# A chunked state-space scan: products of split operands for two plain ones, and 1/sqrt through Ln and Exp

## The chip, the cores and the metric

The kernel runs on one core of one Trainium2 chip. The metric is the device time of one execution in microseconds (us); lower is better. Five engines matter: TensorE (PE, with its weight loads listed as PEld), VectorE (DVE), ScalarE (ACT), GpSimd (POOL), and SyncE (SP), which issues the transfers.

## The reference

A decoder block on 512 positions of width 1024. The part that the change touches is the scan of a Mamba-2 mixer: 32 heads of 64 channels in 4 groups of 8 heads, state size 128, four chunks of 128 positions.

```python
scores = jnp.einsum('bclgn,bcsgn->bgcls', cc, bc)
mmat = scores[:, :, None] * segsum_decay(a_cs)
y_diag = jnp.einsum('bghcls,bcsghp->bclghp', mmat, x)
decay_states = jnp.exp(a_cs[..., -1:] - a_cs)
states = jnp.einsum('bcsgn,bghcs,bcsghp->bcghpn', bc, decay_states, x)
...
def step(h, inp):
    s_c, d_c = inp
    return h * d_c[..., None, None] + s_c, h
...
y_off = jnp.einsum('bclgn,bcghpn,bghcl->bclghp', cc, prev, jnp.exp(a_cs))
...
y = y.reshape(b, seq, D_INNER).astype(h.dtype) * jax.nn.silu(z)
y = rmsnorm(y.reshape(b, seq, SSD_GROUPS, D_INNER // SSD_GROUPS),
            ssd_norm_w.reshape(SSD_GROUPS, D_INNER // SSD_GROUPS))
```

`rmsnorm` multiplies by `rsqrt(mean(x * x) + 1e-5)`, here over the 512 channels of a group. All inputs and the output are float32.

## The kernel before

All activations are kept transposed: 128 channels on the partitions, 512 positions along the free dimension. A matrix is multiplied in units: `unit` loads one 128x1024 block of weights, splits it into a high and a low part (`load_unit`: a cast to float32r on ScalarE, line 141, and a subtraction on VectorE, line 142), and `mm3` adds three products for each of 8 blocks (high x high, high x low, low x high: lines 151, 152, 153), 24 products of 512 columns in all. `split` (lines 121 and 122) does the same for an activation tile.

The scan is `ssd_group(g)`, one generator per group; `run` draws the steps of a group and places units of other matrices between them as fillers (the projections of the next group, the branch product of the group before, the pooling branch). The order of a queue is then set by a scheduler over all instructions, which may move them on ScalarE, VectorE, GpSimd and SyncE; `urgent` gives weight loads a high priority. Buffers are drawn from lists in turn (`S`: 50 tiles of 128x512; `PU`: 3 and `PS`: 5 banks of the accumulator memory; `MT`: 3 decay tiles).

In a group: B is transposed (419) and copied (420) to `bk`; the four score blocks are computed (425). `prepare(c)`, called one chunk ahead, loads the decay rows (433), computes two small exponentials (435, 437), masks on GpSimd (438), does eight exponentials on ScalarE (442), multiplies by the scores (443), transposes x (446), and scales it to `xdt` (448) and, for the first three chunks, to `xd` (454). The chunk's own step multiplies the state (470), forms the chunk's state with one float32 product `st` (474, 128x128 by 128x512), updates it (478, 480, 482), does sixteen small products for the diagonal part (490), and adds, gates and squares on VectorE, ScalarE and GpSimd (497 to 514). `ssum` collects the sums of squares over the four tiles of a group. At the end of a group one float32 product with a matrix of ones (523) sums `ssum` over the partitions and spreads the result; Sqrt (525) and `reciprocal` (527) make `rg`, by which the gated tiles are scaled (532) and then split for the branch product.

ScalarE computes functions from a table; where the next function is in another table, a load (ACT_TABLE_LOAD) stands ahead of it. Silu, Exp, Sqrt and Sigmoid alternate in the scan.

Of the kernel before, what the change touches and what calls it, by code (L numbers as in the profile page):

```python
# [7 lines left out]
F32 = mybir.dt.float32  # L8
F32R = mybir.dt.float32r
AF = mybir.ActivationFunctionType  # L10
ALU = mybir.AluOpType

P = 128
T = 512
# [4 lines left out]
HG = 8  # L19
NC = 4  # L20
# [41 lines left out]
def block_kernel(tc, xT, crow, arow, par, adaT, wstart, wz, wx, wpool_in, wgate, wpw, wbs, wbp, wout, wup, wdn, out):  # L62
# [3 lines left out]
    with (  # L66
# [33 lines left out]
            return par_t[:rows, a:a + n]  # L100

        ident = sb.tile([P, P], F32, name="ident")
        ones = sb.tile([P, P], F32, name="ones")
        eps_t = sb.tile([P, 1], F32, name="eps_t")
        mod = sb.tile([P, 48], F32, name="mod")
        amod = sb.tile([P, 16], F32, name="amod")
# [11 lines left out]
        def split(src):  # L118

            hi, lo = S.get(F32R), S.get(F32R)  # L120
            act.copy(hi, src)
            dve.tensor_tensor(lo, src, hi.bitcast(F32), ALU.subtract)
            return hi, lo
# [25 lines left out]
        def mm3(ps, w, x, start, stop, t0=0, t1=T):  # L149
            (whi, wlo), (xhi, xlo) = w, x  # L150
            pe.matmul(ps, whi, xhi[:, t0:t1], start=start, stop=False)  # L151
            pe.matmul(ps, whi, xlo[:, t0:t1], start=False, stop=False)  # L152
            pe.matmul(ps, wlo, xhi[:, t0:t1], start=False, stop=stop)  # L153
# [256 lines left out]
        def ssd_group(g):  # L410
# [2 lines left out]
            v3 = lambda t: t.rearrange("p (a b) -> p a b", b=64)  # L413
            v4 = lambda t: t.rearrange("p (a b) -> p a b", b=P)
            cdg, decg = cd[g % 2], dec[g % 2]
            bk = S.get()
            ps = PS.get()
            for c in range(NC):
                pe.transpose(ps[:, c * P:(c + 1) * P], bT[:, c * P:(c + 1) * P], ident)
            act.copy(bk, ps)  # L420
            PS.put(ps)
            sc = PS.get()
            for c in range(NC):
# [5 lines left out]
            def prepare(c):  # L429

                cc = slice(c * P, (c + 1) * P)
                m = MT.get()
                sp.dma_start(m, cs_d[heads, cc].partition_broadcast(P))
                if c < 3:
                    act.activation(cdg[:, c, :], m[:, :, P - 1], AF.Exp)  # L435
                    dve.tensor_tensor(decg[:, c, :], m[:, :, P - 1], ncs[:, c, heads], ALU.add)
                    act.activation(decg[:, c, :], decg[:, c, :], AF.Exp)
                pool.affine_select(  # L438
                    m, m, pattern=[[0, HG], [1, P]], compare_op=ALU.is_ge, fill=-1e30, base=0,
                    channel_multiplier=-1)  # L440
                for i in range(HG):
                    act.activation(m[:, i, :], m[:, i, :], AF.Exp, bias=ncs[:, c, g * HG + i:g * HG + i + 1])  # L442
                dve.tensor_tensor(m, m, sc[:, cc].unsqueeze(1).broadcast_to([P, HG, P]), ALU.mult)
                ps = PS.get()
                for i in range(4):
                    pe.transpose(ps[:, i * P:(i + 1) * P], xs[:, i, cc], ident)
                xdt = S.get()
                dve.tensor_tensor(
                    v3(xdt), v3(ps), dtk[:, c, heads].unsqueeze(2).broadcast_to([P, HG, 64]), ALU.mult)
                PS.put(ps)  # L450
                xd = None
                if c < 3:
                    xd = S.get()
                    dve.tensor_tensor(
                        v3(xd), v3(xdt), decg[:, c, :].unsqueeze(2).broadcast_to([P, HG, 64]), ALU.mult)
                return m, xdt, xd

            ready = [prepare(0)]
# [1 line left out]
            for c in range(NC):  # L460
                cc = slice(c * P, (c + 1) * P)
                if c < NC - 1:
                    ready.append(prepare(c + 1))
                    yield
                m, xdt, xd = ready.pop(0)
                yo = None
                if c > 0:
                    yo = PS.get()
                    for i in range(4):
                        pe.matmul(yo[:, i * P:(i + 1) * P], prev[:, i * P:(i + 1) * P], cT[:, cc],  # L470
                                  start=True, stop=True)
                if c < 3:
                    st = PS.get()
                    pe.matmul(st, bk[:, cc], xd, start=True, stop=True)  # L474
                    S.put(xd)
                    nprev = S.get()
                    if c == 0:
                        act.copy(nprev, st)
                    else:
                        dve.tensor_tensor(  # L480
                            v3(nprev), v3(prev), cdg[:, c, :].unsqueeze(2).broadcast_to([P, HG, 64]), ALU.mult)
                        dve.tensor_tensor(nprev, nprev, st, ALU.add)
                        S.put(prev)
                    PS.put(st)
                    prev = nprev
                yd = PS.get()
                for i in range(4):
                    for hh in range(2):
                        o = 64 * hh
                        pe.matmul(  # L490
                            yd[o:o + 64, i * P:(i + 1) * P],
                            xdt[:, i * P + o:i * P + o + 64], m[:, 2 * i + hh, :], start=True, stop=True)
                MT.put(m)
                S.put(xdt)
                y = S.get()
                for i in range(4):
                    dve.scalar_tensor_tensor(
                        y[:, i * P:(i + 1) * P], xs[:, i, cc], col("dskip", 4 * g + i),
                        yd[:, i * P:(i + 1) * P], ALU.mult, ALU.add)
                PS.put(yd)  # L500
                if c > 0:
                    E = S.get()
                    for hh in range(2):
                        sp.dma_start(
                            v4(E)[64 * hh:64 * hh + 64],
                            ecs_d[heads, cc].rearrange("(i t) k -> t i k", t=2)[hh].partition_broadcast(64))
                    dve.tensor_tensor(E, yo, E, ALU.mult)
                    PS.put(yo)
                    dve.tensor_tensor(y, y, E, ALU.add)
                    S.put(E)  # L510
                dve.tensor_tensor(sz[:, :, cc], v4(y), sz[:, :, cc], ALU.mult)
                act.activation(v4(y), sz[:, :, cc], AF.Square)
                pool.tensor_tensor(y[:, :2 * P], y[:, :2 * P], y[:, 2 * P:], ALU.add)
                pool.tensor_tensor(ssum[:, cc], y[:, :P], y[:, P:2 * P], ALU.add)
                S.put(y)
                yield
            S.put(prev, bk)
            PS.put(sc)
            S.put(bT, cT)
            XS.put(xs)  # L520
            yield
            ps = PS.get()
            pe.matmul(ps, ones, ssum, start=True, stop=True)
            rg = S.get()
            act.activation(rg, ps, AF.Sqrt, bias=eps_t, scale=1.0 / T)
            PS.put(ps)
            dve.reciprocal(rg, rg)
            S.put(ssum)
            yield
            ys = []  # L530
# [578 lines left out]
```

## Time and profile before

| what | value |
|---|---|
| time, median of 3 runs | 979.28 us (977.99 to 979.73) |
| profiled execution: span from first to last instruction | 978.1 us (its own time is not given beside the span) |
| mean granted TensorE clock | 0.993 |
| TensorE busy | 958.0 us of the span |
| VectorE, ScalarE, GpSimd busy | 669.1, 522.7, 63.1 us |
| state product (474), on the chain, two records | 0.86 us |
| group sum (523), on the chain, two records | 0.86 us |
| reciprocal (527), four | 3.35 us each |
| table loads on ScalarE | 1.28 us each |

Times in the trace are from the start of the span. Products on TensorE overlap: a product of 512 columns is printed with 0.39 us, but the next one starts 0.23 us later. What a product costs is therefore read from starts, or from the chain that ended last. Float32 products of the plain kind appear as two records each. Names such as `ps<-s,d` say that a tile of the accumulator memory is written from a tile `s` and a weight block `d`.

### The profile page before, as it was taken

The numbers are of one execution on the slowest core, as the hardware profiler recorded it, in microseconds if no ns is written. First come the engines' busy times: TensorE is split into PE (matmuls) and PEld (weight loads), VectorE is DVE, ScalarE is ACT, GpSimd is POOL, SyncE is SP. The second block draws the span as 40 slices with busy tenths as digits, with TensorE's granted clock in tenths as the row PEclk, the third lists the DMA queues.
The fourth block names the chain that finished last, engine by engine and source line by source line (L and its number), as shares of the span: only waits on it lengthen the run. The fifth ranks groups of instructions, "written<-read, shape, count | busy, mean of one in ns | idle before, by whom it ended". The sixth has DMA issues, their size and how long they took to land.

```text
span 978.1 us, 13339 instructions
## 1 busy us (share of the span) xinstructions
PE 958.0 (98%) x5174; PEld 810.9 (83%) x5174; DVE 669.1 (68%) x969; ACT 522.7 (53%) x817; POOL 63.1 (6%) x71
## 2 busy tenths in 40 slices
PE   6999999999999999999999999999999999999997
PEld 5777778888878878788888878998899889889986
DVE  6996969576867786978765576695557556664533
ACT  5388998578438932552422434584157127425632
POOL 0101120120102022200000000000000000000000
PEclk7999999999999999999999999999999999999999
DMA  9747342433343233337885356331144225214002
GB/s 349 285 140 203 101 140 92 125 114 103 112 124 121 87 119 112 126 110 225 268 272 168 114 201 211 99 108 56 64 139 131 65 74 165 86 34 151 22 1 86
DMA packets 62913, 129.62 MB, mean 133 GB/s; under 512 B 4801, under 2 KB 29505, under 8 KB 62850
## 3 DMA queue, kind: packets, MB, share of 16 engines
q1 hardware_dynamic: 62850, 128.77, 40.8%
q8 instruction: 40, 0.66, 0.3%
q14 instruction: 23, 0.19, 0.1%
HBM read 126.53 MB, written 2.23 MB: 132 GB/s over the span
## 4 chain that ended last, share of the span: by engine, by line
PE 85%; ACT 4%; DVE 3%; DMA 3%; issue 2%; POOL 1%; SPq 0%; DVEq 0%; POOLq 0%; ACTq 0%
PE ps L151 22%; PE ps L152 21%; PE ps L153 21%; PE ps L816 12%; PE ps L287 4%; PE ps L490 1%; DMA d<-cs_d 1%; ACT d L141 1%; DMA d<-adaT 1%; DVE d L142 1%; PE ps L474 1%; ACT d L442 1%; ACT L357 1%; PE ps L470 1%; ACT L442 1%
## 5 line engine op out<-in xcount | busy, mean ns | idle before, releaser
L151 PE MATMUL ps<-s,d 128*128 128x512 f32 (+1 forms) x1088 | 416.8, 384 | 3.7 <-ACT pad L549 1.5
L152 PE MATMUL ps<-s,d 128*128 128x512 f32 (+1 forms) x1088 | 411.6, 378 | 0.0
L153 PE MATMUL ps<-s,d 128*128 128x512 f32 (+1 forms) x1088 | 411.3, 378 | 0.0
L151 PEld LDWEIGHTS ps<-s,d 128*128 128x128 f32 x1088 | 204.1, 188 | 47.6 <-issue 2.8
L153 PEld LDWEIGHTS ps<-s,d 128*128 128x128 f32 x1088 | 204.3, 188 | 38.4
L152 PEld LDWEIGHTS ps<-s,d 128*128 128x128 f32 x1088 | 204.3, 188 | 38.2 <-issue 1.1
L141 ACT CAST d<-d 128x1024 fp32r<-128x1024 f32 x89 | 92.8, 1044 | 106.0 <-PE ps L152 92.6
L142 DVE TENSOR_TENSOR d<-d,d 128x1024 fp32r<-128x1024 f32 x89 | 111.2, 1250 | 49.6 <-ACT d L141 49.5
L816 PE MATMUL ps<-s,d 128*128 128x256 f32 x864 | 104.4, 280 | 0.1
L816 PEld LDWEIGHTS ps<-s,d 128*128 128x128 f32 x864 | 102.9, 188 | 1.0 <-ACT ps L836 0.7
L757 ACT CAST d<-d 128x1024 fp32r<-128x1024 f32 x44 | 45.7, 1050 | 90.5 <-PE ps L152 70.1
L757 ACT CAST d<-sz 128x1024 fp32r<-128x1024 f32 x32 | 33.4, 1050 | 71.1 <-PE ps L152 50.1
L996 DVE SCALAR_TENSOR_TENSOR xs<-ps,mod,xs 128x512 f32<-128x512 f32 x29 | 21.5, 751 | 72.4 <-PE ps L153 72.4
L758 DVE TENSOR_TENSOR d<-d,d 128x1024 fp32r<-128x1024 f32 x44 | 53.4, 1224 | 21.9 <-ACT d L757 20.3
L167 DVE CUSTOM_DVE_ANT_0 d<-d,d,par_t 128x1024 f32<-128x1024 f32 x32 | 40.9, 1279 | 20.7 <-DMA d<-adaT 20.7
L758 DVE TENSOR_TENSOR d<-sz,d 128x1024 fp32r<-128x1024 f32 x32 | 39.0, 1224 | 19.8 <-ACT d L757 18.6
L442 ACT ACTIVATE d<-d,ncs 128x128 f32<-128x128 f32 x128 | 41.3, 391 | 11.7 <-POOL d L438 11.5
L353 DVE SCALAR_TENSOR_TENSOR s<-ps,par_t,s 128x511 f32<-128x511 f32 (+2 forms) x54 | 40.1, 743 | 2.4 <-ACT s L351 2.0
L287 PE MATMUL ps<-s,d 128*128 128x512 f32 x144 | 35.5, 397 | 0.5 <-ACT s L275 0.5
L287 PEld LDWEIGHTS ps<-s,d 128*128 128x128 f32 x144 | 26.3, 188 | 8.2 <-ACT s L275 2.9
L758 DVE TENSOR_TENSOR s<-pad,s 128x512 fp32r<-128x512 f32 x34 | 23.2, 688 | 8.0 <-ACT s L757 7.7
L438 POOL TENSOR_SCALAR_AFFINE_SELECT d<-d 128x1024 f32<-128x1024 f32 x16 | 19.9, 1241 | 123.4 <-ACT cd L435 62.4
(209 smaller groups left out, 1020.9 us busy)
## 6 DMA issues: line engine op xcount, KB each, us to landing
d<-adaT SPq DMA_DIRECT2D x32, 512.0 KB, 4.3
d<-wx SPq DMA_DIRECT2D x18, 512.0 KB, 4.1
d<-wdn SPq DMA_DIRECT2D x18, 512.0 KB, 3.9
d<-wz SPq DMA_DIRECT2D x16, 512.0 KB, 3.5
d<-cs_d SPq DMA_DIRECT2D x16, 512.0 KB, 5.9
d<-wbs SPq DMA_DIRECT2D x16, 512.0 KB, 3.4
d<-wgate SPq DMA_DIRECT2D x16, 512.0 KB, 3.5
sz<-wdn SPq DMA_DIRECT2D x14, 512.0 KB, 3.9
```

The source lines that it names most:

```text
L141: act.copy(hi[:, :w], r[:, a:a + w])
L142: (low or dve).tensor_tensor(lo[:, :w], r[:, a:a + w], hi[:, :w].bitcast(F32), ALU.subtract)
L151: pe.matmul(ps, whi, xhi[:, t0:t1], start=start, stop=False)
L152: pe.matmul(ps, whi, xlo[:, t0:t1], start=False, stop=False)
L153: pe.matmul(ps, wlo, xhi[:, t0:t1], start=False, stop=stop)
L167: dve.tensor_tensor_reduce(r, r, cbc, 1.0, col("b_ada", j), ALU.mult, ALU.add, mod[:, j:j + 1])
L287: pe.matmul(first[u], w[u][i // 2], h[k][i % 2], start=k == 0 and i == 0, stop=k == 7 and i == 2)
L353: dve.scalar_tensor_tensor(t[:, sh:], ps[:, :T - sh], w(3 - sh), t[:, sh:], ALU.mult, ALU.add)
L442: act.activation(m[:, i, :], m[:, i, :], AF.Exp, bias=ncs[:, c, g * HG + i:g * HG + i + 1])
L757: act.copy(dst[0], src)
L758: dve.tensor_tensor(dst[1], src, dst[0].bitcast(F32), ALU.subtract)
L816: pe.matmul(ps, x, y, start=start and m == 0 and i == 0, stop=m == 3 and i == 2, skip_group_check=True)
```

## The change

Four things are changed. B is transposed for three chunks instead of four, and kept as a high and a low part. `xd` is split, and the state product becomes an `mm3`. `ssum` is split, and the group sum becomes two products with a float32r matrix of ones. `rg` is computed by Ln (with the same bias and scale) and Exp of -0.5 times that, both on ScalarE, in place of Sqrt and `reciprocal`.

```diff
-        ones = sb.tile([P, P], F32, name="ones")
+        ones_r = sb.tile([P, P], F32R, name="ones")
+        ones = ones_r.bitcast(F32)
...
-            bk = S.get()
+            bk = S.get(F32R), S.get(F32R)
             ps = PS.get()
-            for c in range(NC):
+            for c in range(NC - 1):
                 pe.transpose(ps[:, c * P:(c + 1) * P], bT[:, c * P:(c + 1) * P], ident)
-            act.copy(bk, ps)
+            used = slice(0, (NC - 1) * P)
+            act.copy(bk[0][:, used], ps[:, used])
+            dve.tensor_tensor(bk[1][:, used], ps[:, used], bk[0][:, used].bitcast(F32), ALU.subtract)
...
-                    xd = S.get()
+                    t = S.get()
                     dve.tensor_tensor(
-                        v3(xd), v3(xdt), decg[:, c, :].unsqueeze(2).broadcast_to([P, HG, 64]), ALU.mult)
+                        v3(t), v3(xdt), decg[:, c, :].unsqueeze(2).broadcast_to([P, HG, 64]), ALU.mult)
+                    xd = split(t)
+                    S.put(t)
...
-                    pe.matmul(st, bk[:, cc], xd, start=True, stop=True)
-                    S.put(xd)
+                    mm3(st, tuple(b[:, cc] for b in bk), xd, True, True)
+                    S.put(*xd)
...
-            pe.matmul(ps, ones, ssum, start=True, stop=True)
+            sums2 = split(ssum)
+            for i in range(2):
+                pe.matmul(ps, ones_r, sums2[i], start=i == 0, stop=i == 1)
+            S.put(*sums2)
             rg = S.get()
-            act.activation(rg, ps, AF.Sqrt, bias=eps_t, scale=1.0 / T)
+            act.activation(rg, ps, AF.Ln, bias=eps_t, scale=1.0 / T)
+            act.activation(rg, rg, AF.Exp, scale=-0.5)
             PS.put(ps)
-            dve.reciprocal(rg, rg)
```

The scheduler orders the queues anew. In the changed kernel the lines behind the edits are shifted: 141 becomes 142 (and 151 to 153 become 152 to 154), 121 becomes 122, 385 becomes 386, 435, 437 and 442 become 438, 440 and 445, 512 becomes 517; the group sum is line 530, Ln 533, Exp 534. Table loads are 62 before and 69 now. Three places follow.

TensorE, the end of group 0, before: the last rows of one unit, the group sum, the next unit (`ps` banks, `d` weight blocks, `s` activations).

```order
L151 MATMUL ps_210_1205<-s_84_450,d_208_1201 128x512
L152 MATMUL ps_210_1205<-s_85_451,d_208_1201 128x512
L153 MATMUL ps_210_1205<-s_84_450,d_209_1202 128x512
L523 MATMUL ps_211_1231<-s_133_725,ones 128x512
L151 MATMUL ps_216_1242<-s_42_189,d_214_1238 128x512
L152 MATMUL ps_216_1242<-s_43_190,d_214_1238 128x512
```

The same place now.

```order
L154 MATMUL ps_217_1224<-s_84_450,d_216_1221 128x512
L152 MATMUL ps_225_1266<-s_42_189,d_223_1262 128x512
L530 MATMUL ps_218_1250<-s_219_1251,ones 128x512
L153 MATMUL ps_225_1266<-s_43_190,d_223_1262 128x512
L154 MATMUL ps_225_1266<-s_42_189,d_224_1263 128x512
L152 MATMUL ps_225_1266<-s_48_222,d_223_1262 128x512
L530 MATMUL ps_218_1250<-s_220_1252,ones 128x512
```

One row of the next unit now stands ahead of the group sum, whose second half follows three unit rows later.

ScalarE at the same place, before: from the last Square of group 0 to the Sqrt.

```order
L512 ACTIVATE s_200_1152<-sz_113_584 128x512
L385 ACTIVATE sz_202_1166<-ps_206_1173 128x512
L442 ACT_TABLE_LOAD
L442 ACTIVATE d_243_1397<-d_243_1397,ncs 128x128 x4
L141 CAST d_248_1425<-d_247_1423 128x1024
L385 ACT_TABLE_LOAD
L385 ACTIVATE sz_202_1166<-ps_210_1205 128x512
L525 ACT_TABLE_LOAD
L525 ACTIVATE s_212_1233<-ps_211_1231,eps_t 128x512
```

And now, to the Exp of `rg`.

```order
L517 ACTIVATE s_207_1171<-sz_113_584 128x512
L386 ACTIVATE sz_209_1185<-ps_213_1192 128x512
L445 ACT_TABLE_LOAD
L445 ACTIVATE d_243_1358<-d_243_1358,ncs 128x128
L122 CAST s_219_1251<-s_134_726 128x512
L142 CAST d_262_1458<-d_261_1456 128x1024
L386 ACT_TABLE_LOAD
L386 ACTIVATE sz_209_1185<-ps_217_1224 128x512
L533 ACT_TABLE_LOAD
L533 ACTIVATE s_221_1257<-ps_218_1250,eps_t 128x512
L445 ACT_TABLE_LOAD
L445 ACTIVATE d_243_1358<-d_243_1358,ncs 128x128
```

The cast of `ssum` stands behind a Silu, a table load and an exponential; the Exp of `rg` is the row that follows.

ScalarE earlier in group 0, between the second and the third Square, before: two of the x tiles (357) and exponentials of group 1's decay (442) in turn.

```order
L357 ACT_TABLE_LOAD
L357 ACTIVATE xs_162_902<-s_178_1004 128x512
L442 ACT_TABLE_LOAD
L442 ACTIVATE d_233_1333<-d_233_1333,ncs 128x128 x3
L357 ACT_TABLE_LOAD
L357 ACTIVATE xs_162_902<-s_186_1062 128x512
L442 ACT_TABLE_LOAD
```

And now (358 is the Silu of an x tile, 438 a small exponential).

```order
L358 ACT_TABLE_LOAD
L358 ACTIVATE xs_169_917<-s_174_949 128x512
L142 CAST d_223_1262<-d_222_1260 128x1024
L352 ACTIVATE s_193_1079<-ps_192_1054,par_t 128x512
L358 ACTIVATE xs_169_917<-s_185_1021 128x512
L438 ACT_TABLE_LOAD
L438 ACTIVATE cd_79<-d_255_1426 128x8
L358 ACT_TABLE_LOAD
```

Two x tiles now share a load, and the exponentials of group 1's decay come later. From the small exponential ahead of the first step to the last Square of group 0, ScalarE has 13 loads and 43 exponentials of the decay before, and 11 and 38 now.

More of the change, by code (lines that the diff above doesn't have):

```diff
@@ L516, in ssd_group @@
                 yield
-            S.put(prev, bk)
+            S.put(prev, *bk)
             PS.put(sc)
```

## The prediction

> **What bounds the kernel now.** I read the busy totals first, then busy time by stretch, then what TensorE waited for, then the chain that ended last.
>
> ```profile
> PE 958.0 (98%) x5174; PEld 810.9 (83%) x5174; DVE 669.1 (68%) x969; ACT 522.7 (53%) x817; POOL 63.1 (6%) x71
> ```
>
> TensorE is busy for 98% of the span. A busy TensorE is not yet the bound, so the next view asks where it pauses in the scan (stretch and its length; then busy us and instruction count of TensorE, its weight loads, VectorE, ScalarE and GpSimd; then granted clock, DMA share, GB/s).
>
> ```profile
> 120.00:130.00 10.00, 10.00 (x60) 8.34 (x59) 8.75 (x17) 9.70 (x14) 0.32 (x1) 1.00 0.50 137
> ...
> 130.00:140.00 10.00, 9.14 (x40) 6.92 (x38) 6.54 (x11) 9.06 (x21) 5.55 (x6) 1.00 0.37 109
> ...
> 165.00:225.00 60.00, 60.00 (x320) 48.58 (x319) 37.59 (x59) 42.70 (x76) 11.29 (x12) 1.00 0.40 115
> ...
> 225.00:315.00 90.00, 90.00 (x460) 73.22 (x459) 66.70 (x95) 54.56 (x89) 11.29 (x12) 1.00 0.38 117
> ...
> 375.00:405.00 30.00, 28.46 (x153) 22.85 (x153) 23.01 (x42) 9.84 (x15) 8.95 (x8) 1.00 0.34 110
> ```
>
> In the scan (groups 0 to 3 follow one another from 78 to 430 us) TensorE has no pause except 0.86 us between 130 and 140 and 1.54 us between 375 and 405, at full clock. ScalarE is full only in group 0 (9.70 of 10 us, then 9.06 of 10); in groups 1 and 2 it has a third free. TensorE's waits between 80 and 520 us are just these:
>
> ```profile
> PE ps L151 <- ACT pad L549: 1.5, 1, 1.5
> PE ps L523 <- POOL s L514: 0.9, 1, 0.9
> ```
>
> So between the two waits, and behind them, TensorE's own work sets the time: what is taken off its queue in the scan should come off the end, as long as ScalarE and VectorE still deliver in time. The second wait is a round trip in group 3 (TensorE frees a bank, a copy on ScalarE, sums on GpSimd and VectorE, back); the change puts nothing into the same rows there, so I leave its 1.5 us.
>
> **The state product.** In the chain that ended last (start, us, what) the parts of a scan step on TensorE read:
>
> ```profile
> 164.27 0.86 PE ps L474 x2
> 165.13 1.02 PE ps L490 x16
> 166.15 0.43 PE ps L151
> ...
> 224.41 0.86 PE ps L523 x2
> ...
> 241.64 0.44 PE ps L419 x4
> ...
> 248.91 0.44 PE ps L446 x4
> 249.34 0.24 PE ps L151
> ```
>
> One state product (L474, two records) takes 0.86 us. It becomes three products of split operands through `mm3`, which stand in the same place on TensorE. What one such product costs in a stream is the distance between starts, not its printed duration, since they overlap:
>
> ```profile
> 133.94 0.39 PE L151 MATMUL ps<-s,d 128*128 128x512 f32 x1
> ...
> 137.34 0.39 PE L151 MATMUL ps<-s,d 128*128 128x512 f32 x1
> 137.57 0.39 PE L152 MATMUL ps<-s,d 128*128 128x512 f32 x1
> 137.79 0.39 PE L153 MATMUL ps<-s,d 128*128 128x512 f32 x1
> 139.04 1.13 PE L523 MATMUL ps<-s,ones 128*128 128x512 f32 x2 [0.86 <-POOL s L514]
> ```
>
> The starts 137.34 and 137.57 are 0.23 apart; over a whole unit the distance is 0.227 (137.79 less 133.94, over 17 products). Three take 0.68, so each state product gains 0.18, and twelve (three chunks in four groups) gain 2.16 us.
>
> Two bounds. The first big product after the 64-column products of L490 takes 0.43 instead of 0.23 (166.15). If the same 0.2 were paid behind the L470 products, which stand ahead of eight of the twelve, 1.6 us would go. But the product behind the L446 transposes pays nothing (249.34: 0.24), and L470 has the same 128-column shape, so I take none and keep 1.6 for the range. On the other side nothing makes three products cheaper than 0.68.
>
> **Group sum and transposes.** The product with `ones` (L523, 224.41) takes 0.86 and becomes two at 0.227: 0.41 less, four times 1.62 us. Four transposes of B (241.64) take 0.44; the last chunk's is dropped in each group: 4 x 0.11 = 0.44 us. On TensorE's queue the change thus removes 2.16 + 1.62 + 0.44 = **4.2 us**.
>
> **What it adds elsewhere.** Each group of rows: busy us, mean ns of one, idle before.
>
> ```profile
> L151 PEld LDWEIGHTS ps<-s,d 128*128 128x128 f32 x560 | 105.1, 188 | 26.6 <-issue 2.8 <-ACT pad L549 2.0 <-ACT d L141 0.3
> ...
> L527 DVE RECIPROCAL s<-s 128x512 f32<-128x512 f32 x4 | 13.4, 3354 | 10.4 <-ACT s L525 10.4
> ...
> L122 DVE TENSOR_TENSOR s<-s,s 128x512 fp32r<-128x512 f32 x16 | 10.8, 684 | 1.8 <-ACT s L121 1.8
> ...
> L121 ACT CAST s<-s 128x512 fp32r<-128x512 f32 x16 | 9.9, 621 | 25.2 <-DVE s L562 24.9
> ...
> L512 ACT ACTIVATE s<-sz 128x512 f32<-128x512 f32 x16 | 10.1, 628 | 17.6 <-DVE sz L511 17.5
> ...
> L525 ACT ACTIVATE s<-ps,eps_t 128x512 f32<-128x512 f32 x4 | 2.8, 689 | 0.0
> ```
>
> Sixteen splits (twelve of `xd`, four of `ssum`) add a cast on ScalarE and a subtraction on VectorE each: 16 x 0.62 = 9.9 us and 16 x 0.68 = 10.9 us. The low half of B's transposes adds four subtractions of 384 columns out of PSUM on VectorE, under 0.68 each. The reciprocals go (4 x 3.35 = 13.4), so VectorE stays within 0.3 us of its 669. ScalarE also gets four Exps of `rg` (0.63, as L512), and by the order of the built programs 69 table loads instead of 62. The sum is 9.9 + 2.5 + 7 x 1.28 = 21 us: 544 of 978, hidden beside TensorE, except in group 0. From group sum to `rg`, Sqrt and reciprocal (0.69 + 3.35 = 4.0) become Ln, a load, one exponential that stands between, and Exp (0.69 + 1.28 + 0.3 + 0.63 = 2.9): slightly earlier, and nobody waited there.
>
> **Group 0, the one place without cover.** The split of `ssum` now stands between GpSimd's sum and the group's product, and the casts of `xd` stand in ScalarE's queue ahead of the exponentials.
>
> ```profile
> 84.88 0.21 ACT L437 ACTIVATE dec<-dec 128x8 f32<-128x8 f32 x1
> 85.00 3.32 ACT L442 ACTIVATE d<-d,ncs 128x128 f32<-128x128 f32 x11
> ...
> 136.51 0.63 ACT L512 ACTIVATE s<-sz 128x512 f32<-128x512 f32 x1
> ...
> 143.07 1.28 ACT L525 ACT_TABLE_LOAD   x1
> 144.37 0.69 ACT L525 ACTIVATE s<-ps,eps_t 128x512 f32<-128x512 f32 x1
> ```
>
> A load costs 1.30 from start to next start (143.07 to 144.37), an exponential 0.30 (eleven in 3.32). From 84.88 to the last Square (L512, 136.51 to 137.14) ScalarE's order now holds 11 loads instead of 13, since exponentials were gathered (two places are shown with the change), and 38 exponentials instead of 43, since five for group 1 moved back. Less: 2 x 1.30 + 5 x 0.30 = 4.1. More: three casts, 3 x 0.62 = 1.9, and up to 0.9 of waiting ahead of the first cast, which needs the first half of L454 (84.77, two in 2.18). The last Square moves by d between -1.3 and -2.3; I take d = -1.8.
>
> Behind it ScalarE does one Silu (0.6, sized as L512), a load (1.3), one exponential (0.3) and the cast of `ssum` (0.6), so the high half is there at 137.1 + d + 2.8 = 139.9 + d. TensorE would be at the product at 137.8 + 0.23 less 0.65 (three products of 0.18, one transpose) plus 0.23 for the one unit row that now precedes it: 137.6. The new wait is 2.3 + d = 0.5 us. The old one cost 0.86 of idling plus 0.27, because that L523 took 1.13 instead of 0.86 from its start: 1.13. Gain **0.6 us**. The low half follows four rows later, 0.9 us, for a subtraction of 0.68.
>
> [...] The row here gives 1.30 with no gap behind. [...]
>
> **Is the delay covered in the steps?** The tightest place is the first step:
>
> ```profile
> 84.77 2.18 DVE L454 TENSOR_TENSOR s<-s,dec 128x512 f32<-128x512 f32 x2
> 87.54 1.22 DVE L443 TENSOR_TENSOR d<-d,ps 128x1024 f32<-128x1024 f32 x1 [0.59 <-ACT d L442]
> ...
> 90.34 1.02 PE L474 MATMUL ps<-s,s 128*128 128x512 f32 x2
> 91.29 1.10 PE L490 MATMUL ps<-d,s 128*64 128x128 f32 x16
> ```
>
> The decay matrix (L443) ends at 88.76 and is used by L490 at 91.29: 2.5 us of slack. The cast ahead of its exponentials takes 0.62 plus up to 0.9 of waiting, 1.5 in all; 1 us is left. `xd` itself is wanted at 90.34 and would be split by 85.9 + 0.62 + 0.68 = 87.2. In group 1 the group's sum has room:
>
> ```profile
> 218.97 0.46 POOL L514 TENSOR_TENSOR s<-s 128x128 f32<-128x128 f32 x1
> ...
> 224.25 1.02 PE L523 MATMUL ps<-s,ones 128*128 128x512 f32 x2
> ```
>
> It ends at 219.43 and is used at 224.25; cast and subtraction (1.3 us) fit in 4.8.
>
> **Queues.** On SyncE's queue some loads of the decay for the off-diagonal part (L504) stand a few rows later, ahead of or behind weight loads, and on GpSimd the mask (L438) and the sums (L513, L514) change places in some steps. I give this nothing: weights are cast two to three units ahead and the sum in group 1 has the 4.8 us above. If one of them is late, it shows as a new wait in a step; that is part of the first rival.
>
> **The sum.** 4.2 + 0.6 = 4.8 us. The page gives only the profiled execution's span, 978.1, which would become 973.3; it lies 1.2 below the median of 979.28 and beside the lowest run, 977.99. Against the median I say 979.28 - 4.8 = **974.5 us**.
>
> **Rivals.**
> 1. *The saving is partly lost in the steps*: the first of three split products pays 0.2 behind L470, or small new waits of 1 to 3 us appear, since every queue was reordered. For it: 166.15. Against it: 249.34. The first alone gives 974.5 + 1.6 = 976.1 us. Chance 0.15.
> 2. *ScalarE in group 0 becomes the bound* (the other side). The last Square comes later instead of earlier, because the reordered queue waits for VectorE and GpSimd at other places than before. The wait at the group's product is 2.3 + d, the time changes by (2.3 + d) - 1.13 - 4.2 = d - 3.0. From d = 3.0 on the kernel is slower; with the three casts waiting 1.5 each and no load saved in effect, d = 3 x (0.62 + 1.5) = 6.4 gives 3.4 us more, 982.7 us. For it: ScalarE at 9.7 of 10. Against it: the counts above. Chance 0.07. The same mechanism with d between 1.0 and 5.0 ends within 0.2% of before (2.0 us, about what a measurement of this kernel can tell from no change), say 978.3 at d = 2.0. Chance 0.13.
> 3. *Weight loads come into the open*, so that the split products don't do what they are for. Each product loads its weights (L151 on the weight queue: 188 ns). If a load could not run under the product ahead, three would take 3 x (0.227 + 0.188) = 1.25 instead of 0.86 and two 0.83: 12 x 0.39 = 4.6 lost, 0.1 won; with 0.4 for the transposes and 0.6 in group 0 it gives 979.28 + 4.6 - 0.1 - 1.0 = 982.8 us. Against it: the products at 137.34 and 137.57 start 0.23 apart although each has its own load of 0.188, which would leave 0.04 for the product itself. Chance 0.02. [...]
> 4. *More is won*: group 3's wait of 1.5 us closes because TensorE and VectorE meet there differently, or group 0's goes entirely: 974.5 - 1.5 - 0.5 = 972.5 us. Chance 0.08.
>
> **How the numbers follow.** My forecast has 0.55; its own range is 973.0 to 975.8 (d of -2.3 or less with no wait gives 973.9, d of -1.3 with 1.0 gives 974.9; 0.9 either way for the spread of the runs, 977.99 to 979.73). Range for 8 in 10: from below the fourth rival, 971.8, to where the wait in group 0 has nearly eaten the gain, 978.9; what is left out is rivals 2 (slower) and 3, and the ends of the others. Faster by over 0.2%: 0.55 + 0.15 + 0.08 = 0.78. Within: 0.13. Slower: 0.07 + 0.02 = 0.09.
>
> **What would show it.** In the changed profile: twelve groups of three `mm3` rows on state tiles in about 0.68 in the chain; the group sum at 0.45; weight loads still hidden; TensorE's wait at the first group sum 0 to 1.1 us, and the pad wait in group 3 still near 1.5; VectorE's busy total unchanged, ScalarE's near 544; 69 table loads. I am wrong if TensorE shows a new wait in group 0 of over 3 us, if waits appear in groups 1 and 2, or if the first split product of a step costs 0.4.

## The result, and the profile after

| | before | after |
|---|---|---|
| median of 5 runs | 979.28 us (977.99 to 980.39) | 984.76 us (984.25 to 985.79) |
| profiled execution: its own time, its span | span 978.1 us | 984.25 us, span 982.5 us |
| ratio after to before | | 1.0059, 95% interval 1.0048 to 1.0070 |

The change makes the kernel 5.5 us slower; 974.5 was forecast, with a range of 971.8 to 978.9. The totals of the changed kernel's page:

```profile
PE 959.2 (98%) x5182; PEld 815.3 (83%) x5182; DVE 666.3 (68%) x985; ACT 542.0 (55%) x844; POOL 65.7 (7%) x71
```

These are the totals that were forecast: ScalarE at 542 (forecast 544), VectorE three below 669. They don't tell where 5 us went. The stretches do (same columns as in the prediction):

```profile
120.00:130.00 10.00, 10.00 (x60) 8.34 (x59) 10.00 (x19) 7.93 (x11) 3.31 (x3) 1.00 0.54 142
130.00:140.00 10.00, 7.99 (x35) 6.31 (x35) 6.70 (x12) 9.31 (x17) 3.49 (x4) 1.00 0.36 112
165.00:225.00 60.00, 59.10 (x316) 48.48 (x313) 40.20 (x63) 43.75 (x78) 11.00 (x12) 1.00 0.38 119
225.00:315.00 90.00, 85.78 (x438) 70.12 (x438) 62.67 (x93) 63.12 (x95) 9.21 (x10) 0.98 0.36 109
```

TensorE has lost 4.2 us between 225 and 315, in group 2, where it had no pause at all before; another 0.9 in group 1; and in group 0 (130 to 140) it pauses 2.0 instead of 0.86. Its waits between 80 and 520 us:

```profile
PE ps L152 <- DVE s L354: 5.1, 2, 4.2
PE ps L530 <- ACT s L122: 2.0, 1, 2.0
PE ps L152 <- ACT pad L557: 1.7, 1, 1.7
PE ps L152 <- DVE pad L556: 0.4, 1, 0.4
```

The new one is `L152 <- DVE s L354`: the next unit of TensorE wants an accumulator bank that a convolution's taps (its three shifted multiply-adds on VectorE, line 354) still read. TensorE's rows there:

```profile
262.03 0.60 PE L449 MATMUL ps<-ident,xs 128*128 128x128 f32 x4
266.85 0.47 PE L152 MATMUL ps<-s,d 128*128 128x512 f32 x1 [4.22 <-DVE s L354]
...
267.62 0.46 PE L152 MATMUL ps<-s,d 128*128 128x512 f32 x1
267.87 0.63 PE L153 MATMUL ps<-s,d 128*128 128x512 f32 x1
268.30 0.63 PE L154 MATMUL ps<-s,d 128*128 128x512 f32 x1
...
271.26 0.40 PE L152 MATMUL ps<-s,d 128*128 128x512 f32 x1
```

The pause costs 4.22 us, and more behind it: from 267.87 on the starts are 0.43 apart instead of 0.23, until 271.26. Nine products (267.62 to 271.26) take 3.64 instead of 9 x 0.227 = 2.04, so 1.6 us go to a halved clock. The stretches by microsecond show the grant, third number from the end:

```profile
268.00:269.00 1.00, 1.00 (x4) 0.81 (x3) 1.00 (x2) 0.97 (x3) 0.00 (x0) 0.50 0.48 135
```

What the change was to save on TensorE, it does save. TensorE's rows at a state product in group 1, before:

```profile
164.11 1.02 PE L474 MATMUL ps<-s,s 128*128 128x512 f32 x2
165.06 1.09 PE L490 MATMUL ps<-d,s 128*64 128x128 f32 x16
```

And after, with that group's sum:

```profile
163.77 0.39 PE L152 MATMUL ps<-s,s 128*128 128x512 f32 x1
163.99 0.39 PE L153 MATMUL ps<-s,s 128*128 128x512 f32 x1
164.22 0.39 PE L154 MATMUL ps<-s,s 128*128 128x512 f32 x1
164.54 1.09 PE L495 MATMUL ps<-d,s 128*64 128x128 f32 x16
...
224.60 0.63 PE L530 MATMUL ps<-s,ones 128*128 128x512 f32 x2
225.06 0.39 PE L152 MATMUL ps<-s,d 128*128 128x512 f32 x1
```

From the product's start to the next row it was 0.95 and is now 0.77 (164.54 less 163.77): 0.18 less, as forecast. These are the first products of a group. The eight that stand behind the products with the state (L470, now L475) gain 0.16: from the first of those to the step's next row it was 1.84 and is 1.68. The sum takes 0.46.

**Why the bank comes late.** The convolution row that feeds those taps is on ScalarE. Before (start, us, row) the copy of B, the convolution of the first tile and that of the second stood thus:

```profile
244.34 0.57 ACT L420 COPY s<-ps 128x512 f32<-128x512 f32 x1
...
249.70 0.77 ACT L351 ACTIVATE s<-ps,par_t 128x512 f32<-128x512 f32 x1
...
255.80 0.77 ACT L351 ACTIVATE s<-ps,par_t 128x512 f32<-128x512 f32 x1
```

And after:

```profile
249.52 0.47 ACT L422 CAST s<-ps 128x384 fp32r<-128x384 f32 x1
250.02 1.28 ACT L445 ACT_TABLE_LOAD   x1
251.31 0.70 ACT L445 ACTIVATE d<-d,ncs 128x128 f32<-128x128 f32 x2
252.95 0.62 ACT L122 CAST s<-s 128x512 fp32r<-128x512 f32 x1 [0.94 <-DVE s L457]
...
254.43 0.76 ACT L352 ACTIVATE s<-ps,par_t 128x512 f32<-128x512 f32 x1
258.33 0.62 ACT L122 CAST s<-s 128x512 fp32r<-128x512 f32 x1 [3.14 <-DVE s L457]
...
259.93 1.28 ACT L358 ACT_TABLE_LOAD   x1
261.22 0.63 ACT L358 ACTIVATE s<-s 128x512 f32<-128x512 f32 x1
261.76 0.76 ACT L352 ACTIVATE s<-ps,par_t 128x512 f32<-128x512 f32 x1
```

Two things are seen. The copy of B is already 5.2 us late; and behind it the new casts of `xd` (L122), one of which waits 3.14 us for VectorE, and a table load stand ahead of the convolution rows. The first row is 4.7 us late, the second 6.0 (261.76 instead of 255.80). A third delay is on VectorE. Before, the last tap of the second tile ended at 259.64, 3.1 us behind its row, and TensorE took the bank only at 262.56, so 2.9 us were to spare:

```profile
258.90 0.74 DVE L353 SCALAR_TENSOR_TENSOR s<-ps,par_t,s 128x509 f32<-128x509 f32 x1
...
262.56 0.47 PE L151 MATMUL ps<-s,d 128*128 128x512 f32 x1
```

Now a sum of the branch product (L405) and the scaling of the state (L485) stand between the taps, and the last tap ends at 266.70, 4.2 us behind its row:

```profile
263.50 0.68 DVE L405 TENSOR_TENSOR s<-s,ps 128x512 f32<-128x512 f32 x1
...
264.76 1.29 DVE L485 TENSOR_TENSOR s<-s,cd 128x512 f32<-128x512 f32 x1
265.97 0.73 DVE L354 SCALAR_TENSOR_TENSOR s<-ps,par_t,s 128x509 f32<-128x509 f32 x1
```

So 6.0 us from ScalarE and 1.1 from VectorE, less the 2.9 to spare, make the pause of 4.2. Most of ScalarE's part comes from the stretch ahead, busy time of each engine between 230 and 250 us, before and after:

```profile
230.00:250.00 20.00, 20.00 (x100) 16.79 (x99) 16.73 (x18) 13.78 (x19) 0.00 (x0) 1.00 0.32 106
```

```profile
230.00:250.00 20.00, 20.00 (x100) 16.77 (x99) 10.04 (x13) 19.78 (x26) 0.00 (x0) 1.00 0.24 80
```

ScalarE had 13.78 of 20 us to do and now has 19.78. From the root of the group's factor (231.61 before, 232.66 after) to the copy of B it loads 2 tables before and 6 after, since SiLU of z (L386) and single decays (L445) now alternate in its queue. The copy's 5.2 us are made up of the root, which is itself 1.05 late, four loads at 1.30 (5.2), and two decays and the Exp of the factor (1.1), less some 2.2 us in which ScalarE was idle there before.

### The profile page after: what moved, and what is told of

The parts are those of the page before. It is cut to its first block, busy times and chain, and to the rows that moved or that the text cites. A ratio compares the mean times of both kernels' runs of the same rounds, so it can differ in the third digit from the quotient of the medians.

```text
span 982.5 us, 13403 instructions
## 1 busy us (share of the span) xinstructions
PE 959.2 (98%) x5182; PEld 815.3 (83%) x5182; DVE 666.3 (68%) x985; ACT 542.0 (55%) x844; POOL 65.7 (7%) x71
## 4 chain that ended last, share of the span: by engine, by line
PE 73%; ACT 9%; DVE 7%; issue 7%; DMA 3%; POOL 1%; DVEq 0%; SPq 0%; POOLq 0%; ACTq 0%
PE ps L152 18%; PE ps L153 18%; PE ps L154 18%; PE ps L824 12%; PE ps L288 3%; ACT d L142 2%; DMA d<-cs_d 2%; DVE s L354 1%; DVE d L143 1%; ACT L445 1%; ACT d L445 1%; ACT L358 1%; DMA d<-adaT 1%; ACT L386 1%; POOL pad L566 1%
## 5 line engine op out<-in xcount | busy, mean ns | idle before, releaser
L152 PE MATMUL ps<-s,d 128*128 128x512 f32 (+1 forms) x1088 | 416.0, 383 | 9.6 <-DVE s L354 5.1
L152 PEld LDWEIGHTS ps<-s,d 128*128 128x128 f32 x1088 | 204.5, 188 | 53.7 <-ACT d L445 4.4
L765 ACT CAST d<-d 128x1024 fp32r<-128x1024 f32 x44 | 45.7, 1051 | 89.5 <-PE ps L153 70.4
L445 ACT ACTIVATE d<-d,ncs 128x128 f32<-128x128 f32 x128 | 42.0, 392 | 5.4 <-POOL d L441 5.1
L354 DVE SCALAR_TENSOR_TENSOR s<-ps,par_t,s 128x511 f32<-128x511 f32 (+2 forms) x54 | 40.0, 743 | 3.1 <-ACT s L352 2.8
L122 ACT CAST s<-s 128x512 fp32r<-128x512 f32 x32 | 19.6, 617 | 35.2 <-DVE s L570 24.4
```

The costliest lines, as they stand in the source:

```text
L354: dve.scalar_tensor_tensor(t[:, sh:], ps[:, :T - sh], w(3 - sh), t[:, sh:], ALU.mult, ALU.add)
L765: act.copy(dst[0], src)
```

## The experiments

Ratios are against the kernel before, run on the same chip. "Stages" are read from the starts of the first score product (L425 before) of each group: group 0 to 1, 1 to 2, 2 to 3, and from group 3 to the end of the span; the last also holds TensorE's waits behind the scan, of which the larger ones add up to 1.6 us before, 1.4 after and 0.6 in e8. "Copy" and "row" are the starts of B's copy and of the second convolution row of group 2 on ScalarE, "pause" is TensorE's wait for the taps there. Groups 1 and 2 of e11 and e12 start 12 to 15 us later, so their copy and row don't compare with the rest.

| kernel | median, us | ratio, 95% interval | stages, us | copy | row | pause |
|---|---|---|---|---|---|---|
| before | 979.28 | | 82.1, 90.5, 90.5, 645.6 | 244.34 | 255.80 | 0 |
| after | 984.76 | 1.0059 (1.0048 to 1.0070) | 82.5, 90.7, 95.8, 645.0 | 249.52 | 261.76 | 4.22 |
| e1 sum alone | 978.36 | 0.9999 (0.9990 to 1.0008) | 82.5, 90.3, 90.6, 644.0 | 249.73 | 258.64 | 0.17 |
| e2 state alone | 977.91 | 0.9989 (0.9980 to 0.9998) | 82.4, 90.3, 89.9, 645.9 | 246.70 | 256.92 | 0 |
| e3 convolution first | 977.13 | 0.9981 (0.9972 to 0.9990) | 82.9, 89.6, 90.0, 644.2 | 246.43 | 257.18 | 0.17 |
| e4 the same, before | 978.82 | 1.0000 (0.9991 to 1.0009) | 82.1, 90.5, 90.5, 645.8 | 243.31 | 254.77 | 0 |
| e5 splits, Sqrt | 981.00 | 1.0017 (1.0008 to 1.0026) | 82.3, 89.5, 94.6, 643.9 | 247.83 | 259.27 | 3.22 |
| e6 cast on GpSimd | 985.71 | 1.0076 (1.0064 to 1.0089) | 85.1, 89.5, 95.4, 646.9 | 250.95 | 262.29 | 3.90 |
| e7 cast on VectorE | 981.74 | 1.0030 (1.0020 to 1.0041) | 81.3, 91.1, 93.2, 646.3 | 248.87 | 260.55 | 1.79 |
| e8 = e3 and e6 | 976.78 | 0.9978 (0.9969 to 0.9987) | 82.5, 89.5, 89.5, 643.3 | 245.81 | 254.35 | 0 |
| e9 no decays' Exp, after | 976.14 | 0.9971 (0.9961 to 0.9981) | 82.3, 89.5, 89.5, 643.7 | 241.30 | 254.44 | 0 |
| e10 the same, before | 977.86 | 0.9987 (0.9978 to 0.9996) | 81.0, 90.5, 90.5, 645.2 | 241.12 | 253.81 | 0 |
| e11 Tanh | 989.95 | 1.0110 (1.0097 to 1.0124) | 91.4, 89.6, 89.6, 644.0 | 254.59 | 267.74 | 0 |
| e12 Tanh, convolution first | 991.36 | 1.0126 (1.0112 to 1.0140) | 93.4, 89.6, 89.6, 645.3 | 256.41 | 268.22 | 0 |
| e13 = e8, sum of group 0 whole | 975.50 | 0.9964 (0.9951 to 0.9976) | 82.0, 89.5, 89.5, 644.1 | 245.93 | 253.84 | 0 |
| e14 = e3, sum of group 0 whole | 976.96 | 0.9980 (0.9971 to 0.9989) | 82.4, 90.3, 90.2, 644.0 | 246.50 | 257.25 | 0.38 |

**One part at a time.** e1 keeps the split of the sum with Ln and Exp, and takes the state product back to float32 (with `xd` whole and B's four transposes as before):

```diff
-                    mm3(st, tuple(b[:, cc] for b in bk), xd, True, True)
+                    pe.matmul(st, bk[:, cc], xd, start=True, stop=True)
```

> The changed kernel without the state product's part: B's transposes and xd stay whole, the state product is the one float32 product of before; the split group sum and Ln with Exp stay. Theory A (the splits of the state product's operands put casts and subtractions ahead of the convolution's rows on ScalarE and VectorE, the convolution holds its bank longer, TensorE pauses): no pause in groups 1 and 2, TensorE saves 4 x 0.4 = 1.6 us, so 977.7 us, 976.5 to 978.7, against 979.3 before. Theory B (Ln and Exp bring table loads, ScalarE falls behind): the 4.2 us pause of group 2 is still there, 982 us or more.

e2 keeps the split of the state, and takes the sum, Sqrt and reciprocal back:

```diff
-                pe.matmul(ps, ones_r, sums2[i], start=i == 0, stop=i == 1)
...
+            pe.matmul(ps, ones, ssum, start=True, stop=True)
...
```

> The state product's part alone: group sum, Sqrt and reciprocal as before. Theory A: TensorE saves 12 x 0.15 + 0.4 = 2.2 us, the pauses stay in part (ScalarE has 64 table loads here, and none between the two convolution rows of group 2, so a pause shorter than 4.2 us): 979 to 983 us. Theory B: no pause, 977 us.

e1 came out near theory A and refutes B as stated: Ln and Exp with the split of the sum lose nothing (nor is a gain clear of noise). e2 was below what A said. So neither part alone makes the pause; the two together do, and A was not yet a theory of why. The copy and the row say how: in e1 the copy of B is as late as in the changed kernel (the same loads, 8 between 228 and 250 us), but no cast of `xd` stands between it and the convolution, and the pause is 0.17, just closed. In e2 the casts stand there, one waiting 4.26 us for VectorE, but the copy is 2.8 us earlier, and there is no pause either. In both, VectorE's rows among the taps are as before: the last tap ends 3.1 and 2.8 us behind its row, against 4.2 in the changed kernel. Each part uses up some of the 2.9 us; the pause comes where the sum exceeds them.

e2's profiled run paused 1.95 us in group 3 (1.54 before), and its granted clock fell there (0.50 from 404 to 406), so its last stage is 645.9 and not 644:

```profile
402.99 0.77 PE L152 MATMUL ps<-s,d 128*128 128x512 f32 x1 [1.95 <-ACT pad L554]
403.56 0.63 PE L153 MATMUL ps<-s,d 128*128 128x512 f32 x1
...
406.75 0.39 PE L152 MATMUL ps<-s,d 128*128 128x512 f32 x1
```

**The convolution's rows first.** e3 gives the convolution's activation and taps the priority that the weight loads have; e4 does it to the kernel before.

```diff
+            with tc.high_priority() if urgent[0] else nullcontext():
                 act.activation(t, ps, AF.Identity, bias=col("conv_b", j), scale=w(3))
```

> The whole change, and the convolution's first activation and three taps, which read the bank, get the high priority that weight loads have. Theory A: the pauses that end on a convolution tap go (4.2, 0.9 and the slow clock behind the first), TensorE's 3.9 us stay won, less what group 0 still waits (1 us more than before): 975.5 to 977.5 us. Theory B: as the changed kernel, 983 us or more, since 67 table loads stay.

> The kernel before with the same priority for the convolution, so that e3 can be read against it. TensorE had no wait on a convolution there, so theory A and B both say no gain from this but what group 0's wait of 0.9 us gives: 978 to 979.6 us.

Order alone turns 5.5 us lost into 2 won, with all casts, subtractions, Ln and Exp kept; on the kernel before it does nothing. Groups 1 and 2 now take 89.6 and 90.0 instead of 90.5 each. The rows that gave way cost something: TensorE now waits 0.9 us once for a decay matrix (L447 there).

**Sqrt back, both splits kept** (Ln and Exp replaced by `AF.Sqrt` and `dve.reciprocal`):

> Both splits stay; the group's factor is again Sqrt on ScalarE and a reciprocal on VectorE. In the written order of ScalarE the stretch of group 2 in which the changed kernel paused is the same: B copy, table load, two decays, split cast of the state's operand, convolution row, second split cast, table load, SiLU, second convolution row. Theory A (the splits reorder ScalarE's queue and the queue's order makes the pause, whatever function takes the root): 983 to 986 us, with the pause of some 4 us in group 2. Rival B (Ln and Exp with their table loads make the loss): 976 to 980, no pause in group 2.

Between the two, and neither was right: the pause stays (3.22), so Ln and Exp are not needed for it, but they are worth 3.8 us of the 984.76. Without them copy and row are 1.7 and 2.5 us earlier, and by the stages 1.2 us come back in group 1, 1.2 in group 2 and 1.1 behind. Against e2 only the split of the sum is added, with its cast and subtraction: the row is 2.4 us later and the taps again take 4.2 us.

**The cast off ScalarE's queue.**

```diff
-                    xd = split(t)
+                    xd = S.get(F32R), S.get(F32R)
+                    pool.tensor_copy(xd[0], t)
+                    dve.tensor_tensor(xd[1], t, xd[0].bitcast(F32), ALU.subtract)
```

> The changed kernel with the upper half of the state's split operand cast on GpSimd instead of ScalarE (12 casts). Theory A: the convolution's second row in group 2 no longer stands behind a cast that waits 3.14 us for VectorE, so it starts about 3.7 us earlier; the pause of 4.22 falls to 0 to 1 us and the half clock behind it (1.6 us) goes: 978 to 981. Rival C (the table loads and decays ahead of that row are enough for the pause): 983 to 985, pause over 3 us. Rival D (VectorE's subtraction, now behind GpSimd's cast, holds up the taps instead): 981 to 986, with VectorE idle ahead of the subtraction in its rows.

e7 has `dve.tensor_copy` in the second added line.

> The changed kernel with that cast on VectorE (12 casts of about 0.5 us, 6 us more there). Theory A: as with GpSimd, the cast no longer waits in ScalarE's queue: 978 to 981, pause in group 2 under 1.5 us; the wait at the sum of group 0, where VectorE was full, up to 1 us longer than the 2.0 us of the changed kernel. Rival C (table loads and decays alone): 983 to 985.

Both lie above what theory A allowed, in time and in the pause, and refute it in its simple form. e6 has the pause that rival C gave and 0.7 us more than its range; the sign of rival D is missing in group 2, where VectorE does not idle ahead of the subtraction. (The profiled execution of e6 took 987.13, with a halved clock in groups 0, 2 and 3: a mean of 0.66 from 140 to 145, 0.78 and 0.88 in the two stretches from 265 to 275, 0.66 from 410 to 415.) e7 falls between A and C, and has other waits besides: 1.3 us in group 1 on a tap (0.9 in the changed kernel), and 1.2 in group 2 and 1.0 in group 3 on a subtraction (L461 there), which the changed kernel has not. With no cast in the queue, ScalarE waits just as long for the taps of the first tile, ahead of its SiLU (e6, ScalarE):

```profile
254.28 0.77 ACT L352 ACTIVATE s<-ps,par_t 128x512 f32<-128x512 f32 x1
...
260.46 1.28 ACT L358 ACT_TABLE_LOAD   x1 [3.48 <-DVE s L354]
```

So the cast's 3.14 us in the changed kernel are not the cause: its SiLU would have waited for these taps, which end at 258.96, without any cast. What is late is all that follows the copy of B (250.95 here, with six loads between the root and it, as in the changed kernel). In e7 copy and row are 0.6 and 1.2 us earlier than in the changed kernel; its casts among the taps took 0.41 to 0.42 us each on VectorE, and its pause of 1.79 has no half clock behind it (1.00 from 260 to 275). e8 is e3 with the edit of e6:

> The kernel of the run in which the convolution's rows went first (977.1 us), with the cast on GpSimd besides. ScalarE and its table loads (67 to 63) are lighter. Theory A: group 0 gets back part of the 1 us that it lost to ScalarE's queue: 975 to 977. Rival D (VectorE waits for GpSimd's casts): 977 to 979.5.

There the pause is gone and group 0 takes 82.5 instead of 82.9, as A had said; the intervals of e3 and e8 overlap.

**The table loads.** That left the loads ahead of the copy as the cause to test (theory A2). e9 leaves the decays' exponentials out, e10 does so in the kernel before:

```diff
...
-                    act.activation(m[:, i, :], m[:, i, :], AF.Exp, bias=ncs[:, c, g * HG + i:g * HG + i + 1])
+                    act.activation(m[:, i, :], m[:, i, :], AF.Identity, scale=0.0, bias=ncs[:, c, g * HG + i:g * HG + i + 1])
```

> The changed kernel with the scan's decays (the two small rows of a chunk and the eight that make its mask) taken by Identity with scale 0 in place of Exp: the decays are left out, every row, size and cast of the splits stays. ScalarE then has 20 table loads instead of 69. Theory A2 (the reordered queue lets Exp and SiLU alternate; the loads, 1.30 us each, put the B copy of group 2 off from 244.3 to 249.5 us, and the splits' casts behind them use up the rest of the slack): the B copy of group 2 at 245 or earlier, no pause in group 2, time 973.5 to 976.5. Rival A1 (the cast that waits for VectorE ahead of the convolution row is enough by itself): a pause over 2 us stays in group 2, 980 to 984.

> The kernel before with the same decays left out in the same way: 16 table loads instead of 62. Theory A2: before, the loads are covered in groups 1 to 3, so only group 0, where ScalarE is full, can gain: 977 to 979. If it falls to 975 or less, the loads cost the kernel before as well, and the difference between e9 and this run, not e9 alone, is what the splits are worth.

e9 has every cast and subtraction of the changed kernel and no pause in groups 1 and 2. TensorE's waits between 80 and 520 us:

```profile
PE ps L152 <- ACT pad L557: 1.7, 1, 1.7
PE ps L530 <- ACT s L122: 1.4, 1, 1.4
PE ps L530 <- DVE s L123: 0.2, 1, 0.2
```

ScalarE between 230 and 250 us does 12.12 instead of 19.78:

```profile
230.00:250.00 20.00, 20.00 (x100) 16.76 (x98) 16.66 (x21) 12.12 (x17) 0.00 (x0) 1.00 0.28 93
```

The same edit gives the kernel before 1.3 us (979.14 in that comparison; by the stages 1.1 in group 0), and the changed one 8.6. So the pause goes with the loads, but the loads alone don't make it. e1 and e2 have the six loads between root and copy as well and no pause over 0.17; e3 and e8 have them too, and with the convolution's rows first it is gone. The rest is the order behind the copy, on ScalarE and among VectorE's taps. What each of these rows costs is read from the traces: each edit lets the scheduler order all queues anew (in e9 only the rows of before stand among the taps), so no run changes one of them alone. With the loads gone from both kernels the change is worth 1.7 us (976.14 against 977.86).

e11 takes most of the loads away with nothing left out:

```diff
...
-            act.activation(o, t, AF.Silu)
+            act.activation(o, t, AF.Tanh)
+            dve.scalar_tensor_tensor(o, o, 1.0, t, ALU.add, ALU.mult)
...
```

> The changed kernel with each SiLU of the convolutions and of z as half the operand times one plus tanh of it (the convolution's parameters halved once at the start, the epsilon of the group's root times 4): Tanh shares a table with Exp in the built program, so 14 table loads instead of 69 (55 times 1.30 = 71 us less on ScalarE), and 40 more rows of about 0.68 us (27 us) on VectorE. Nothing is left out. Theory A2: no pause in group 2, 973.5 to 977. Rival D (VectorE, which was full in group 0, becomes the bound): waits for VectorE of over 3 us in all in the groups, 979 to 984. Rival A1: pause over 2 us in group 2, 980 to 984.

> The same, with the convolution's rows first in the written order and the group's root by Sqrt and reciprocal again: 13 table loads. Theory A2: 973 to 976.5, the fastest of the runs so far. Rival D: 978 to 983, with waits for VectorE in groups 0 and 1.

The pause is gone, as A2 said, and groups 1 and 2 take 89.6 us, as without the decays. The times, 989.95 and 991.36, lie above every range given, rival D's too: group 0, where VectorE was full, takes 9 us more in e11 (TensorE waits 3.5 us for VectorE, 3.2 at the sum, and runs twice for 3.4 us at half clock: a mean of 0.66 from 85 to 90 and from 150 to 155), and the start 4 more, since the halving of the parameters waits for their transfer ahead of other work in VectorE's queue, which is a fault of the experiment:

```profile
10.29 0.22 DVE L222 TENSOR_SCALAR par_t<-par_t 128x120 f32<-128x120 f32 x1 [9.12 <-DMA par_t<-par]
```

Tanh rows follow Exp rows without a load: in e11 Exp starts at 231.14 and 243.42, Tanh at 232.91 and 247.02, and of the two loads between 228 and 272 us one stands ahead of Ln (240.12), the other ahead of the Exp behind it (242.12). The built program has 14 loads instead of 69.

**Group 0.** Was it the split of the sum itself, which stands last there? e13 and e14 take it back in group 0 alone:

```diff
+            if g == 0:
+                pe.matmul(ps, ones, ssum, start=True, stop=True)
...
```

> The kernel of the run e8 (convolution rows first, cast on GpSimd, 976.8 us) with the group sum of group 0 alone as one whole product again (0.86 us instead of 2 of 0.227, a cast and a subtraction fewer ahead of it). Theory A3 (the loss in group 0 is the split of the sum itself: TensorE waits there for ScalarE's cast of the sum, 1.8 us in e8): the group's sum stands 0.4 to 1 us earlier against the group's start, no wait at it above 1 us, 975.5 to 976.5. Rival E (the loss comes from the splits ahead of it, which keep ScalarE and VectorE full in group 0): the wait stays, now for GpSimd's sum, and the 0.41 us that the split saves is lost: 977 to 977.5.

> The same edit on the kernel of the run e3 (convolution rows first, cast on ScalarE, 977.1 us; its wait at that sum was 1.1 us). Theory A3: 976.3 to 977. Rival E: 977.2 to 977.8.

e13 is the fastest kernel of the study, 3.4 us below before. From the first scores to the sum group 0 takes 69.8 us, as before (69.8), instead of 70.4 in e8; in e14 it takes 70.2 instead of the 70.8 of e3. The wait in e13 is now for GpSimd's last term:

```profile
PE ps L152 <- ACT pad L563: 1.6, 1, 1.6
PE ps L532 <- POOL s L522: 1.2, 1, 1.2
```

So the split of that one sum costs 0.5 to 0.7 us there, by its cast; the median moves by 1.3 from e8 to e13 (the intervals overlap) and by 0.2 from e3 to e14. A3 is right on the place and the times; its bound of 1 us for the wait was missed by 0.2, and the wait for GpSimd is what rival E said. And since TensorE had by then 3 x 0.18 = 0.54 us less to do than before but is no earlier, that much is still lost in group 0 to what feeds it.

## Why the prediction was wrong

**TensorE's 4.2 us** were right. In a group without pauses (group 1 of e5, e6, e8, e9 and e13) the stage is 89.5 instead of 90.5 us: 1.0, where 3 x 0.18 + 0.41 + 0.11 = 1.06 was forecast. Most of the difference is what two of a group's three state products lose behind the products with the state, 0.02 each and not 0.2, so that part of rival 1 is out. The split products start 0.23 apart (163.77, 163.99, 164.22) although each has its own weight load of 0.19 (L152 on the weight queue: 191 ns), so weight loads stayed hidden and rival 3 is out.

**The failed step** is the one under "What it adds elsewhere": "544 of 978, hidden beside TensorE, except in group 0". The 544 was right to 2 us; "hidden" was read from ScalarE's mean over 60 and 90 us, "a third free". Seven loads more in all looked like 9 us spread over the kernel. In fact four more than before stood between group 1's root and group 2's copy of B, where ScalarE went from 13.78 to 19.78 of 20 us, and the convolution rows came up to 6.0 us late. In place of nothing this cost a pause of 4.22 us and 1.6 at half clock in group 2, and 0.9 in group 1. The convolution's rows put first (e3, 984.76 to 977.13) or the decays' loads taken out (e9, 976.14) remove it, with every split kept. The part "Is the delay covered in the steps?" followed the cast to the decay matrix, to `xd` and to group 1's sum. It did not follow ScalarE's queue to the convolution rows, which hold the bank of TensorE's next unit. "Queues", too, priced the reordering at nothing on SyncE and GpSimd and left ScalarE's and VectorE's own order out; on VectorE, whose total was forecast as unchanged, two rows among the taps made up 1.1 us of the pause. The written order that was at hand shows the loads; only the term was not made.

**Group 0**, d. The count of loads and exponentials was taken for the motion of the last Square, d = -1.8. It was -0.4: 136.51 before, 136.10 after.

```profile
133.33 1.28 ACT L358 ACT_TABLE_LOAD   x1 [0.65 <-DVE s L354]
...
136.10 0.62 ACT L517 ACTIVATE s<-sz 128x512 f32<-128x512 f32 x1
...
138.51 0.40 ACT L445 ACTIVATE d<-d,ncs 128x128 f32<-128x128 f32 x1
138.81 0.60 ACT L122 CAST s<-s 128x512 fp32r<-128x512 f32 x1
```

From 84.8 us to that Square ScalarE worked 3.0 us less, more than the 2.2 or so that the count gave, but it idled 2.6 more (5.1 instead of 2.5). Of this it waited 3.6 us for VectorE (0.65 of them in the first row), against 0.2 before; VectorE was at 10.00 of 10 between 120 and 130, 8.75 before. With the measured d the formula 2.3 + d gives a wait of 1.9; it was 2.01. The formula held, its input did not.

**Rivals.** Rival 1 named the place ("small new waits", "it shows as a new wait in a step") but gave it 1 to 3 us and looked for it at weight loads, masks and sums. Rival 2 had the right engine; its mechanism, a queue that waits for VectorE at other places, did act in group 0, where it cost some 1.5 us, but most of the loss came in group 2. The condition "if waits appear in groups 1 and 2" is what happened.

**The balance**, by the stages of the two profiled executions. Forecast were 1.66 saved in group 0 (1.06 and 0.6), 1.06 in groups 1 and 2 each, 0.95 behind: 4.7. Measured were 0.3, 0.2 and 5.3 lost and 0.6 won: 5.1 lost, by the unrounded starts. The 9.8 between them are: 5.8 in group 2 (pause and half clock), 0.9 for group 1's pause, 1.5 for group 0's wait (2.01 against the 0.5 forecast), 0.5 for group 3's (1.65 and 0.44 against 1.54). The last 1.1 I can't place line by line.

## What to carry to other kernels

An engine's share over a long stretch doesn't show whether more work on it hides: follow its written order row by row to the next row that frees something the bounding engine waits for, and count table loads in that piece, not in the kernel. Two additions that each fit in the slack need not fit together; try them apart and together. When a scheduler reorders, the cure can be a priority on the rows that hold a bank (7.6 us here), with the arithmetic left as it is.

## What the runs showed of the hardware

In these runs the length of a pause of TensorE did not tell whether a half clock followed. A pause of 1.95 us (e2, 401.04 to 402.99) was followed at once by half clock, from 403.04 to 406.46 (granted clock 0.50 from 404 to 406); 2.01 us in the changed kernel's group 0 and 1.65 in its group 3 were followed by none (1.00 from 136 to 145 and from 408 to 415); 4.22 us was followed by it only 1.0 us after TensorE had started again, from 267.81 to 271.22 (0.50 from 268 to 271). Both times the half clock lasted 3.4 us. Nine products took 3.64 us there in the changed kernel and 3.76 in e2 (402.99 to 406.75) instead of 2.04, so it cost 1.6 and 1.7 us. What makes the clock fall is not shown: none of the runs was made to test it.
